# Side work of an attention stage: a list of counts per step, row sums moved between stages, and the order of two kinds of side jobs exchanged

## The chip, the cores and the metric

The kernel runs on one core of one Trainium2 chip. The metric is the device time of one execution in microseconds (us), as the median of several runs. Five engines work in parallel, each through its own queue in order: TensorE (PE in the profile; PEld is its weight load), VectorE (DVE), ScalarE (ACT), GpSimd (POOL) and SyncE (SP), which here issues most transfers.

## The reference

One inference step of two layers over 128 context tokens and 512 latent tokens, width 1024, in float32. Layer 0 is gated grouped-query attention (16 query heads, 4 key heads, head size 64), layer 1 a bidirectional gated linear recurrence. Each layer first modulates its input with shift and scale from a conditioning vector, and multiplies its output by a gate from the same vector:

```python
def _adaln(cond, w, b):
    mod = jax.nn.silu(cond.astype(jnp.float32)) @ w.astype(jnp.float32) + b.astype(jnp.float32)
    mod = mod.astype(cond.dtype)
    return jnp.split(mod, 3, axis=-1)
...
        sh_p, sc_p, g_p = _adaln(c_ctx, ada_w[i], ada_b[i])
        sh_s, sc_s, g_s = _adaln(c, ada_w[i], ada_b[i])
        hp = xp * (1.0 + sc_p) + sh_p
        hs = xs * (1.0 + sc_s) + sh_s
...
    q = _rms_norm(q.reshape(B, L, N_HEADS, HEAD_DIM), q_gain)
...
    gated = o.reshape(B, L, ATTN_WIDTH).astype(jnp.float32) * jax.nn.silu(g.astype(jnp.float32))
```

The change concerns three products with small results: the shift and scale of layer 1 (here called row sums), the gates of both layers (here called the gates' products), and the queries of layer 0.

## The kernel before, in words

All 640 tokens (five tiles of 128) are worked on together. Matrix products are made in three terms from a high and a low half of each operand (`whi`, `wlo`, `hhi`, `hlo`).

**Lead-in** (`lead_in`, L753). After the keys and values, PE makes the first of four query chunks (256 columns, four heads) and then the attention's SiLU gate path: 16 half tiles of 24 matmuls each over 320 tokens (`feat_mms`, L346, L853), four weight chunks (6 to 9) of four half tiles. After each half tile ScalarE writes its SiLU (L854). Between the half tiles stand the steps that norm, rotate and split the first queries (`q_job`, L803, ending in L694, which PE's transposes L702 read) and split the keys (`k_split`). Also after each half tile stands one job of row sums (L861) as long as there are any.

**Row sums** (`ada_cols`, L331). A job is one of 16 pieces, a 128x1024 slice of the transposed weight of layer 1's shift and scale. VectorE multiplies it with the SiLU of each of the two conditioning vectors, spread over the partitions in `silb`, and sums along the row: two instructions, L335. The product itself goes to a place that nobody reads (`spill`). Twelve of the 16 jobs are in the lead-in, with raw pieces in two buffers of their own (`adaraw`, loaded at L840 on SP's queue, the first two ahead, each further one when a job is done) and the spill in a part of `gs` that is written last. The last four (`COLS_LATE`) come later, with pieces from the common ring of three raw buffers and the spill in a ring of two slots (`s2`) that the key and query splits use too.

**Gates' products** (`ada_gen`, L315). For each layer four steps of 16 small matmuls (L284) with an add on VectorE (L321), then four small stores to memory. For layer 0 the result is then read back, spread over the partitions, into `gate0` (`gate_load`, L311), which takes over the memory of `silb`; the output projection of layer 0 needs it (L1174).

**Attention** (`att_gen`, L1001) has 36 units, nine for each of the four query chunks; each has steps that make scores, transpose probabilities and apply them to the values. Beside it runs the side work (`Side`, L60): query chunks 1, 2 and 3 (`q_gen`, L713), weights of the output projection, and splits of the attention's result. Each query chunk has a filler that it steps at places of its own: the last four jobs of row sums in chunk 1, the products of gate 0 in chunk 2, those of gate 1 in chunk 3 (L1125). `weave` (L87) takes one step of the attention, then side steps at a fixed rate of 0.62 a step. Before the first scores of a chunk, all that is left of its query chunk is forced (`side.until`, L1013).

**What sets the order.** All up to L1248 is one block whose instructions a planner puts in order on each engine: the source's order is the priority, but an instruction whose inputs are ready in the planner's own model may go ahead of earlier ones. `keep_in_program_order` (`pin`) ties an instruction to the one written before it on its engine; adaraw's loads are pinned on SP. `issue_after(ins)` puts what is written inside it behind `ins` in the queue of the engine of `ins`; elsewhere in the kernel it is given an instruction of the same engine as what is tied. The loads of raw pieces follow one list (`order`, L395 to L402), two pieces ahead (`pump`, L197).

## Time and profile before

| what | value |
|---|---|
| median of 3 runs | 842.29 us (842.24 to 848.55) |
| the profiled execution | 844.78 us |
| its span in the profile | 843.0 us |
| mean granted clock of TensorE | 0.99 |
| TensorE busy | 808.0 us of the span |
| VectorE, ScalarE, GpSimd busy | 559.9, 386.5, 215.8 us |
| row sums in the lead-in, in the attention | 24 and 8 instructions |
| gates' products | 128 matmuls, from 190.1 to 286.1 us |

The span runs from the first to the last instruction; the execution's own time has a little around it. Times in the rows are in us from the start of the span. In a row of the order of time stand start, duration, engine, line, operation, output and inputs, shape and count; in brackets the idle time of the engine before it and what ended that. In a table of windows stand the length and the busy time of each engine with its number of instructions, then the clock that TensorE was granted (1.00 is full), the share of the transfer engines and GB/s. Matmuls overlap, so their durations add up to more than the time they take.

### The profile page before, as it was taken

What the parts mean: (1) busy time and instruction counts of PE and PEld (TensorE: products, weight loads), DVE (VectorE), ACT (ScalarE), POOL (GpSimd) and SP (SyncE); (2) the same over time, 40 slices, a digit from 0 to 9 for tenths busy, and PEclk for the clock granted to TensorE, in tenths of its full rate; (3) what the DMA queues carried; (4) which work ended last, traced back from release to release, by engine and by line L of the source; (5) the groups of instructions that cost most, each with busy time, mean ns of one, the idle gap of its engine ahead of it and who ended that gap; (6) DMA issues with size and microseconds to landing.
All of it is one profiled execution on the core that took longest, in us unless ns stands there. A gap on an engine that the chain in (4) does not pass through costs nothing.

```text
span 843.0 us, 19206 instructions
## 1 busy us (share of the span) xinstructions
PE 808.0 (96%) x8025; PEld 729.2 (87%) x8025; DVE 559.9 (66%) x996; ACT 386.5 (46%) x782; POOL 215.8 (26%) x261
## 2 busy tenths in 40 slices
PE   8999899989999988999999999999999999999994
PEld 6789799878878766888999999999999999998774
DVE  4568882795657674776438575767668575858477
ACT  2252354674656776222434444435434544445232
POOL 0123001443344833010001304143333314121121
PEclk9999899999999999999999999999999999999998
DMA  9944451114151230630322322231322312324041
GB/s 325 397 145 165 151 175 52 51 54 148 51 200 51 101 100 1 225 125 35 108 69 68 103 72 82 83 109 51 107 89 83 99 61 89 120 65 157 23 161 75
DMA packets 34326, 93.28 MB, mean 111 GB/s; under 512 B 5040, under 2 KB 12224, under 8 KB 34240
## 3 DMA queue, kind: packets, MB, share of 16 engines
q1 hardware_dynamic: 23568, 74.10, 25.9%
q0 software_dynamic: 4768, 14.18, 5.4%
q10 hardware_dynamic: 5904, 3.78, 1.5%
q8 instruction: 63, 1.03, 0.5%
q14 instruction: 23, 0.19, 0.1%
HBM read 82.85 MB, written 9.19 MB: 109 GB/s over the span
## 4 chain that ended last, share of the span: by engine, by line
PE 82%; DVE 9%; ACT 2%; DMA 2%; issue 2%; POOL 1%; SPq 0%; DVEq 0%; ACTq 0%; POOLq 0%
PE rps L1319 7%; PE rps L1320 7%; PE rps L1321 7%; PE vgps L1309 5%; PE vgps L1311 5%; PE vgps L1310 5%; PE pot L896 4%; PE outp L1158 4%; PE outp L1160 3%; PE outp L1159 3%; PE pt L982 3%; PE lv L1452 2%; PE acc L536 2%; PE gps L349 2%; PE sc L869 2%
## 5 line engine op out<-in xcount | busy, mean ns | idle before, releaser
L1319 PE MATMUL rps<-h1hi,rhi 128*128 128x320 f32 x368 | 118.4, 322 | 0.0
L1320 PE MATMUL rps<-h1lo,rhi 128*128 128x320 f32 x368 | 113.9, 309 | 0.0
L1321 PE MATMUL rps<-h1hi,rlo 128*128 128x320 f32 x368 | 113.8, 309 | 0.0
L975 POOL TENSOR_SCALAR p<-p,rc 128x640 f32<-128x640 f32 x64 | 58.8, 921 | 116.6 <-DVE rc L974 102.3
L1319 PEld LDWEIGHTS rps<-h1hi,rhi 128*128 128x128 f32 x368 | 69.2, 188 | 1.3
L1320 PEld LDWEIGHTS rps<-h1lo,rhi 128*128 128x128 f32 x368 | 69.3, 188 | 0.0
L1321 PEld LDWEIGHTS rps<-h1hi,rlo 128*128 128x128 f32 x368 | 69.1, 188 | 0.0
L241 DVE TENSOR_TENSOR rlo<-raw,rhi 128x1024 fp32r<-128x1024 f32 x32 | 45.0, 1409 | 33.8 <-ACT rhi L240 33.8
L964 DVE TENSOR_REDUCE nm<-sc 128x1 f32<-128x640 f32 x64 | 52.0, 818 | 23.2 <-PE sc L870 22.8
L1480 POOL COPY At<-near 32x160 f32<-32x160 f32 x32 | 14.0, 438 | 196.8 <-DVE near L1442 195.8
L969 ACT ACTIVATE p<-sc,nm 128x640 f32<-128x640 f32 x64 | 51.2, 802 | 27.2 <-DVE nm L964 19.3
L240 ACT CAST rhi<-raw 128x1024 fp32r<-128x1024 f32 x32 | 33.6, 1049 | 52.0 <-PE rps L1320 48.8
L1430 ACT COPY kc<-A 128x640 f32<-128x640 f32 x40 | 32.2, 806 | 54.4 <-DVE A L1461 50.5
L1309 PE MATMUL vgps<-rhi,h1hi 128*128 128x256 f32 x180 | 51.5, 286 | 0.0
L1310 PE MATMUL vgps<-rlo,h1hi 128*128 128x256 f32 x180 | 50.9, 283 | 0.0
L1311 PE MATMUL vgps<-rhi,h1lo 128*128 128x256 f32 x180 | 50.9, 283 | 0.0
L982 PE MATMUL pt<-small,p 128*128 128x128 f32 x320 | 48.6, 276 | 1.4 <-ACT pts L874 0.9
L869 PE MATMUL sc<-kk,X 128*128 128x320 f32 x128 | 42.6, 343 | 6.1 <-ACT p L969 6.0
L874 ACT COPY pts<-pt 128x512 f32<-128x512 f32 x64 | 35.8, 591 | 24.4 <-PE pt L982 24.1
L982 PEld LDWEIGHTS pt<-small,p 128*128 128x128 f32 x320 | 37.1, 140 | 7.8 <-issue 5.3
L1309 PE MATMUL vgps<-wspare,h1hi 128*128 128x256 f32 x140 | 41.8, 298 | 0.0
L896 PE MATMUL pot<-pts,vv 128*64 128x256 f32 x320 | 38.9, 386 | 2.4 <-DVE pts L874 2.4
(301 smaller groups left out, 2423.6 us busy)
## 6 DMA issues: line engine op xcount, KB each, us to landing
raw<-in_rec_w_in SPq DMA_DIRECT2D x40, 512.0 KB, 3.7
raw<-in_ada_m SPq DMA_DIRECT2D x16, 512.0 KB, 8.0
raw<-in_attn_w_in SPq DMA_DIRECT2D x16, 512.0 KB, 4.2
raw<-in_ada_s SPq DMA_DIRECT2D x16, 512.0 KB, 4.4
adaraw<-in_ada_c SPq DMA_DIRECT2D x12, 512.0 KB, 3.8
raw<-in_attn_w_out SPq DMA_DIRECT2D x8, 512.0 KB, 4.1
raw<-in_rec_w_out SPq DMA_DIRECT2D x8, 512.0 KB, 3.5
x1d<-y SPq DMA_DIRECT2D x5, 512.0 KB, 2.6
```

The source lines that it names most:

```text
L869: nc.tensor.matmul(out, X[:, h, t0:t0 + P], kk[:, c, k0:k1], start=True, stop=False)
L896: nc.tensor.matmul(pot[j * HD:(j + 1) * HD, :CW], vv[:, slot, c * HD:(c + 1) * HD], moving[j], start=first, stop=last)
L964: nc.vector.tensor_reduce(nm[:, 0:1], sc[:, :, :320], AX.XY, ALU.max, negate=True)
L969: return nc.scalar.activation(halves(p[:]), sc[:, :, :320], AF.Exp, bias=nm[:, 0:1], accum_out=su[:, 0:1])
L975: nc.gpsimd.tensor_scalar(p, p, rs[:, 0:1], 1.0, ALU.mult, ALU.mult)
L982: nc.tensor.transpose(pt[:, i * 256 + q * P:i * 256 + (q + 1) * P], ps[q][:, (k0 + i) * P:(k0 + i + 1) * P], ident)
L1309: nc.tensor.matmul(out, h1hi[:, k, t], hi, start=(k == 0), stop=False)
L1310: nc.tensor.matmul(out, h1hi[:, k, t], lo, start=False, stop=False)
L1311: nc.tensor.matmul(out, h1lo[:, k, t], hi, start=False, stop=(k == KT - 1))
L1319: nc.tensor.matmul(ps[:, j, :320], hi[:, k, :], h1hi[:, k, t], start=(k == 0), stop=False)
L1320: nc.tensor.matmul(ps[:, j, :320], hi[:, k, :], h1lo[:, k, t], start=False, stop=False)
L1321: nc.tensor.matmul(ps[:, j, :320], lo[:, k, :], h1hi[:, k, t], start=False, stop=(k == KT - 1))
```

## The change

1. In the lead-in, eleven jobs of row sums and not twelve. They are made by a generator that stops after each of a job's two sums. `ROWS_AT` says how many sums stand after each half tile: none after the first four, one after the fifth and sixth, two after the seventh to fifteenth; what is left follows the last. Each sum stands in an `issue_after` with the latest SiLU. The spill is in `gs` up to the twelfth half tile, then in the `s2` ring. The next raw piece is still loaded when a job is done.
2. The five other jobs go beside query chunk 3, one sum a step; then comes the load of `gate0`. The products of gate 0 go beside chunk 1 and those of gate 1 beside chunk 2; the list of loads is exchanged alike.
3. `FILL_AT` says at which places of a query chunk its filler is stepped: the token tile of the unit and a letter for the half of a token tile after which it stands, or `e` for the end of the unit. Before, it was one step at the start of chunks 2 and 3, one in each unit, and the rest at the end.
4. `SIDE_AT` is a digit for each of the attention's 189 steps: the number of side steps behind it, in place of the rate 0.62.

```diff
+FILL_AT = {1: '0a0b0e2e4e', 2: '0b0e2e4e', 3: '0b0e4e'}
...
-SIDE_B = 0.62
+SIDE_AT = (
+    "0101101011111000110110101101011011010110111001101021010010110110"
+    "1001011010210101200101002011110100110101101002011000121110001101"
+    "0110110101101002002110010110101101102002011101000001201101011")
...
-COLS_LATE = 4
+COLS_LATE = 5
+ROWS_AT = (0, 0, 0, 0, 1, 1, 2, 2, 2, 2, 2, 2, 2, 2, 2, 0)
...
-def weave(main, side, ratio):
-    acc = 0.0
-    for _ in main:
-        acc += ratio
-        while acc >= 1.0:
-            acc -= 1.0
+def weave(main, side, steps):
+    for n, _ in enumerate(main):
+        for _ in range(int(steps[n]) if n < len(steps) else 1):
             side.step()
...
         yield
-        if layer == 0:
-            gate[0] = gsp.tile([P, 2, D], F32, tag="gate", name="gate0")
-            gate_load(0, nc.gpsimd)
-
-    def ada_cols(job, raw, spill):
+
+    def ada_cols(job, raw, spill, after):
...
         for c in range(2):
-            nc.vector.scalar_tensor_tensor(spill, raw, 1.0, silb[:, c, :], ALU.mult, ALU.mult,
-                                           accum_out=shsc[1][:, s, ft, c:c + 1])
+            with tc.issue_after(after()) if after else ExitStack():
+                nc.vector.scalar_tensor_tensor(spill(), raw, 1.0, silb[:, c, :], ALU.mult, ALU.mult,
+                                               accum_out=shsc[1][:, s, ft, c:c + 1])
+            yield
...
+    def spare():
+        return prep.tile([P, D], F32, tag="s2", name="spill", bufs=2)
+
     def cols_gen():
         for job in COLS[len(COLS) - COLS_LATE:]:
-            ada_cols(job, take(("ada_c",) + job), prep.tile([P, D], F32, tag="s2", name="spill", bufs=2))
+            yield from ada_cols(job, take(("ada_c",) + job), spare, None)
             pump()
-            yield
+        gate[0] = gsp.tile([P, 2, D], F32, tag="gate", name="gate0")
+        gate_load(0, nc.gpsimd)
...
-        order.extend(ada_pieces(c - 1) if c else [("ada_c",) + job for job in COLS[len(COLS) - COLS_LATE:]])
+        order.extend(ada_pieces(c) if c < 2 else [("ada_c",) + job for job in COLS[len(COLS) - COLS_LATE:]])
...
-        if c > 1:
-            next(fill)
-            yield
+        spots = {FILL_AT[c][i:i + 2] for i in range(0, len(FILL_AT[c]), 2)}
         pend = None
         for tt0, n in UNITS:
-            ps = yield from tok_unit(w, tt0, n, "qmm")
+            ps = None
+            gen = tok_unit(w, tt0, n, "qmm")
+            step = 0
+            while ps is None:
+                try:
+                    next(gen)
+                except StopIteration as e:
+                    ps = e.value
+                    break
+                step += 1
+                yield
+                if f"{tt0}{'0abcd'[step]}" in spots:
+                    next(fill, None)
+                    yield
...
-            next(fill, None)
-            yield
+            if f"{tt0}e" in spots:
+                next(fill, None)
+                yield
...
+        silus = []
+
+        def spill():
+            return gs[:, KT - 2:, :].rearrange("p a b -> p (a b)")[:, :D] if len(silus) <= 12 else spare()
+
+        def cols_steps():
+            while raws:
+                yield from ada_cols(*raws.popleft(), spill, lambda: silus[-1])
+                cols_load()
+
+        cgen = cols_steps()
...
-                    nc.scalar.activation(gs[:, 2 * (ch - 6) + mt, t0:t1], ps[:, :320], AF.Silu)
+                    silus.append(nc.scalar.activation(gs[:, 2 * (ch - 6) + mt, t0:t1], ps[:, :320], AF.Silu).ins)
...
-                    if raws:
-                        ada_cols(*raws.popleft(), gs[:, KT - 2:, :].rearrange("p a b -> p (a b)")[:, :D])
-                        cols_load()
+                    for _ in range(ROWS_AT[step - 1]):
+                        next(cgen, None)
...
-        assert not raws
+        drain(cgen)
...
-        yield from q_gen(c, Xs[c], ada_gen(c - 2) if c > 1 else cols_gen())
+        yield from q_gen(c, Xs[c], ada_gen(c - 1) if c < 3 else cols_gen())
...
-    weave(att, side, SIDE_B)
+    weave(att, side, SIDE_AT)
```

## The prediction

> **What bounds the kernel now.** I read the page's busy shares, then busy time by stretch, then the chain of waits, then single engines in order of time.

> ```profile
> PE 808.0 (96%) x8025; PEld 729.2 (87%) x8025; DVE 559.9 (66%) x996; ACT 386.5 (46%) x782; POOL 215.8 (26%) x261
> PE 82%; DVE 9%; ACT 2%; DMA 2%; issue 2%; POOL 1%; SPq 0%; DVEq 0%; ACTq 0%; POOLq 0%
> ```

> TensorE is the bound: 808.0 of 843.0 us busy, 82% of the chain. The change touches none of its work, so it can only win back idle time, 35 us in all, and only in the stage it edits. The next rows show that stage: two pieces of the lead-in, then the attention, cut about where its query chunks are made (first, second and last chunk, then what follows).

> ```profile
> 86.24:91.78 5.54, 1.39 (x11) 1.07 (x9) 5.54 (x11) 1.70 (x4) 0.00 (x0) 0.73 0.43 155
> 91.78:97.10 5.32, 5.32 (x24) 5.32 (x25) 5.32 (x10) 2.10 (x3) 0.00 (x0) 0.64 0.21 85
> 141.00:190.00 49.00, 44.44 (x351) 38.71 (x349) 42.11 (x95) 32.08 (x72) 23.01 (x21) 1.00 0.18 58
> 190.00:240.00 50.00, 49.43 (x429) 40.66 (x429) 31.33 (x71) 29.16 (x66) 19.97 (x23) 1.00 0.32 114
> 240.00:292.00 52.00, 50.64 (x440) 42.43 (x439) 33.82 (x71) 32.14 (x74) 30.56 (x32) 1.00 0.33 112
> 292.00:338.00 46.00, 39.94 (x293) 29.46 (x293) 26.95 (x58) 32.75 (x70) 18.15 (x22) 1.00 0.15 47
> ```

> After each window's length come the busy times of PE, weight load, DVE, ACT and POOL, then the granted clock. PE idles 4.15 us in the first window and runs at a clock of 0.64 in the second. It idles 4.56 us beside the first chunk, where DVE has its fullest stretch (42.11 of 49), 0.57 beside the second, 1.36 beside the last and 6.06 after it.

> **Part 1: the row sums leave the first four half tiles.** DVE's order of time, the transposes that wait for it, and the loads:

> ```profile
> 82.45 0.69 DVE L615 TENSOR_TENSOR qn<-pmm,rq 128x512 f32<-128x512 f32 x1 [0.85 <-POOL rq L191]
> 83.06 1.21 DVE L335 SCALAR_TENSOR_TENSOR gs<-adaraw,silb 128x1024 f32<-128x1024 f32 x1
> ...
> 85.40 1.22 DVE L335 SCALAR_TENSOR_TENSOR gs<-adaraw,silb 128x1024 f32<-128x1024 f32 x1
> ...
> 87.75 1.22 DVE L335 SCALAR_TENSOR_TENSOR gs<-adaraw,silb 128x1024 f32<-128x1024 f32 x1
> ...
> 89.49 0.69 DVE L694 TENSOR_TENSOR qs<-r,qs 128x512 fp32r<-128x512 f32 x1
> ```
> ```profile
> 90.33 1.23 PE L702 MATMUL qps<-identr,qs 128*128 128x128 f32 x8 [3.92 <-DVE qs L694]
> ...
> 98.27 0.80 PE L702 MATMUL qps<-identr,qs 128*128 128x128 f32 x8
> ```
> ```profile
> 58.75 0.90 SPq L840 DMA_DIRECT2D adaraw<-in_ada_c  x2
> 62.64 11.67 SPq L219 DMA_DIRECT2D raw<-in_attn_w_in  x2
> 76.05 13.28 SPq L840 DMA_DIRECT2D adaraw<-in_ada_c  x4
> 89.38 8.68 SPq L219 DMA_DIRECT2D raw<-in_attn_w_in  x2
> ```
> ```profile
> 82.92 0.44 ACT L854 ACTIVATE gs<-gps 128x320 f32<-128x320 f32 x1 [3.08 <-PE gps L351]
> 86.44 0.44 ACT L854 ACTIVATE gs<-gps 128x320 f32<-128x320 f32 x1 [3.08 <-PE gps L351]
> ```

> The first query tile's chain (82.45 to 89.49) has three row sums between its links; PE's transposes stand in its in-order queue and wait 3.92 us for the last link. Then PE is slow: a half tile takes 86.44 - 82.92 = 3.52 us, but 5.32 in the window at clock 0.64, 1.80 more. The eight transposes take 1.23 against 0.80, and 0.2 of idle follows: 0.6. This place costs 3.92 + 1.80 + 0.6 = 6.3 us.

> ROWS_AT begins the first pair of sums at half tiles 5 and 6. SP's queue holds this up: the third adaraw load is now written in half tile 7, behind the weight pieces which now issue at 89.38 to 98.06, perhaps 6 us earlier without the stall. So job 3 cannot run before about 92. Only the four sums of jobs 1 and 2, whose data come with the loads of 58.75, could run earlier. The chain without the three sums: each holds DVE some 1.15 us, 3.5 us together; the last link then ends near 86.3, PE being ready at 86.24. Gain 6.3; bounds: 0, if the four sums take the places of the three, and 6.3.

> I count nothing on the tie: it names a Silu, on ACT, while the sums run on DVE, and issue_after orders only what shares the named instruction's engine. If it were a true wait, DVE would stand behind a Silu up to a half tile (3.52 us), and with it the key splits and PE's transposes after them.

> Nine jobs follow from about 92 until the attention starts. Two sums a half tile at 1.23 are 2.45 of 3.52 us; DVE's spare time there hides them (0.82 busy between 130 and 140, one row below). The extra buffer for the last sums shares its slots with the key splits: cost nothing while that spare time is there; if it is gone, the attention's first maxima are late by a sum, 1.2 us.

> ```profile
> 130.00:140.00 10.00, 10.00 (x72) 9.99 (x71) 0.82 (x1) 3.90 (x9) 0.00 (x0) 1.00 0.01 2
> ```

> **Part 2: the first chunk gets products for row sums.** The chain of waits in this stretch, and the sums and products by themselves:

> ```profile
> 144.42 1.21 DVE spill L335 x2
> ...
> 146.37 1.14 DVE spill L335 x2
> ...
> 182.76 1.33 DVE spill L335 x2
> ...
> 185.55 1.15 DVE spill L335 x2
> 186.72 3.35 DMA raw<-in_ada_s
> ```
> ```profile
> L335 DVE SCALAR_TENSOR_TENSOR spill<-raw,silb x8: 1208/1214/1747, 144.3 to 185.5; 128x1024 f32<-128x1024 f32 x8
> ```
> ```profile
> 200.26 1.07 PE L284 MATMUL adaps<-raw,sil 128*32 128x256 f32 x16
> ...
> 273.92 0.42 DVE L321 TENSOR_TENSOR acc<-acc,adaps 128x256 f32<-128x256 f32 x1
> ```

> Four of the eight sums lie on the chain, 4.83 us. They go, and four products of sixteen matmuls (1.07 us each) come: PE's 4.3 us fill into its 4.56 of idle time, DVE falls from 42.11 by 8 x 1.3 and rises by four adds of 0.42, to about 33 of 49. The products only move: first chunk +4.3, second as before (ada1 for ada0), last chunk -4.3. So the stretch stays near 49 and the last one loses 4.3. Bounds: 0 if the idle time is the start of the softmax and not DVE, 4.56 if all goes. I take 4.3, since the sums are on the chain.

> The products' loads come earlier in SP's queue, behind the eleventh adaraw load; bounds 0 and one landing (4.4, below) for each of four steps. I take 0: the planner places a product where it expects its data.

> **Part 3: ten sums beside the last chunk.** DVE there goes from 33.82, less 4 x 0.42, plus 10 x 1.23, to 44.4 of about 47.7 us. Seven of them are written behind the last query split, six steps being forced at its deadline (two before). But DVE's order is not the source's: modA, written behind the whole attention, runs where its data are ready:

> ```profile
> 190.89 0.16 DVE L1090 TENSOR_TENSOR modA<-shsc,lnc 128x16 f32<-128x16 f32 x1
> ```
> ```profile
> PE qps L702 <- DVE qs L694: 1.0, 1, 1.0
> ```

> So sums spread into DVE's gaps from when their raws land. The cost lies between 0 and the first chunk's 4.83 us. The nearest row is the stretch's own: PE once waits 1.0 us there for DVE. I add one more such wait: +1.0. Whoever waits behind a sum: maxima, reciprocals and probability copies, then ACT's exponentials and PE.

> The gate load moves to the end of these sums; POOL issues it, and its data are needed only at the output projection, past 338: nothing, while some 40 us lie between. Its issue waits for the last sum, and POOL's scalings queue behind it; at one sum at most, inside the 1.0.

> **Part 4: counts and places.** I stepped both orders through: the same attention steps, the same deadlines, side steps moved by one or two places. After the last chunk there is no query product left to fill PE, so its 6.06 us stay. I take 0, bounds -4 (two thirds of that idle time) and +3 (about half as much again as PE idles beside the three chunks, 4.56 + 0.57 + 1.36 = 6.5).

> **The sum.** -6.3 - 4.3 + 1.0 + 0 = -9.6 us. The profiled execution took 844.78 us (span 843.0 and 1.8 around it), so 835.2; it lay 2.5 above the median of 842.29, so as a median 832.7.

> [...] DVE beside POOL:

> ```profile
> L335 DVE SCALAR_TENSOR_TENSOR gs<-adaraw,silb x24: 1214/1224/1226, 71.6 to 122.0; 128x1024 f32<-128x1024 f32 x24
> ```
> ```profile
> L975 POOL TENSOR_SCALAR p<-p,rc x64: 788/800/2217, 143.8 to 330.2; 128x640 f32<-128x640 f32 x64
> ```

> Where POOL is idle (the lead-in) all 24 sums take 1.21 to 1.23; beside POOL's scalings one of eight took 1.747, and a scaling grew from 0.800 to 2.217. POOL is fuller in the last chunk (30.56 of 52) than in the first (23.01 of 49). [...]

> **Rivals.** First, the last chunk gives back what the first gains: DVE at 93% there, and ten sums against scalings that take up to 1.4 us longer. Part 3 costs the first chunk's 4.83 and not 1.0: 832.7 + 3.8 = 836.5. For it: the swap is nearly symmetrical. Against: DVE has 18 us to spare there, and X3 does not wait for a sum.

> Second, the row sums are not held back: with a void tie the planner puts jobs 1 and 2 into the chain's gaps. Then the stall stays and only parts 2 and 3 count: 842.29 - 3.3 = 839.0. Against: those four now run before 82.45, while DVE waits for POOL's rq.

> Third, slower: the products come too early for their data. Loads queue on SP behind adaraw loads that wait for sums, and PE's queue is in order:

> ```profile
> raw<-in_ada_s SPq DMA_DIRECT2D x16, 512.0 KB, 4.4
> ```

> If each of the first chunk's four steps waits a whole landing of 4.4 us, 17.6 - 9.6 = +8.0: 850.3. It decides from 2.4 us a step. For it: the chain already has 3.35 of such a load at 186.72. Against: that load waited for a sum's buffer, which no longer stands before a product.

> Fourth, the counts also clear part of what follows the last chunk, part 4 at -4: 828.7.

> **How the numbers follow.** Main 0.55 at 832.7, its own range 829.5 to 836; first rival 0.18, second 0.08, third 0.06, fourth 0.13. A measurement of this kernel can tell about 1% from no change, 833.9 and 850.7 here. Main lies below 833.9 in about two of three cases (0.37); with the fourth 0.50 faster. Slower by over 1% is half of the third and a little for what I miss: 0.04. The rest, 0.46, is within 1%. The range 828 to 840 leaves out the third rival and the edges of the others.

> **What would show it.** Part 1: the wait of qps for qs near 86 to 90 gone, clock 1.00 through the lead-in, no adaraw sum of job 3 before 92; wrong if the wait is still over 1 us. Part 2: PE idle beside the first chunk under 1.5 us with adaps there, no spill on its chain. Part 3: PE idle beside the last chunk under 2.5; wrong if spill rows stand on its chain for over 2 us. Part 4: idle after it still 5 to 7. The forecast is wrong above all if the lead-in's stall returns at another link, such as the key splits.

## The result, and the profile after

The changed kernel takes 838.25 us as a median of 7 runs (836.37 to 839.39), the kernel before 845.39 in the runs beside it. The ratio is 0.9918, with a 95% interval of 0.9899 to 0.9938: faster by 0.8%. The three runs from which the forecast started (842.29) lay low; the sets of runs beside the experiments had medians of 845.09, 843.66, 844.46 and 845.31. So the fair comparison is by ratio: forecast 835.2 / 844.78 = 0.9886, measured 0.9918; or -9.6 us forecast, -6.9 measured.

The page of the changed kernel, busy shares and the chain:

```profile
PE 806.7 (97%) x8025; PEld 727.9 (87%) x8025; DVE 563.3 (67%) x996; ACT 386.6 (46%) x782; POOL 212.5 (25%) x261
PE 82%; DVE 9%; issue 3%; ACT 2%; DMA 1%; POOL 1%; SPq 0%; DVEq 0%; ACTq 0%; POOLq 0%
```

TensorE is the bound as before. To see where the time went, both traces are cut at the same events: first and last matmul of the half tiles, last transposes of the first, second and last query chunk, first matmul of the output projection. The kernel before, then the changed one; columns as in the prediction's windows:

```profile
72.17:140.78 68.61, 64.46 (x448) 64.00 (x447) 48.65 (x79) 27.99 (x53) 4.47 (x1) 0.95 0.40 131
140.78:187.32 46.54, 43.01 (x342) 37.55 (x342) 39.65 (x89) 31.19 (x70) 22.14 (x19) 1.00 0.15 47
187.32:237.59 50.27, 48.66 (x423) 40.82 (x423) 32.11 (x75) 27.83 (x63) 19.86 (x23) 1.00 0.35 122
237.59:292.34 54.75, 53.39 (x462) 43.99 (x463) 36.06 (x74) 34.55 (x79) 31.88 (x33) 1.00 0.32 111
292.34:336.82 44.48, 38.42 (x284) 28.13 (x282) 26.15 (x57) 31.57 (x69) 16.79 (x20) 1.00 0.15 48
336.82:843.00 506.18, 492.21 (x5496) 459.23 (x5496) 336.18 (x546) 209.17 (x412) 107.50 (x150) 0.99 0.30 94
```
```profile
71.49:134.50 63.01, 62.58 (x448) 62.05 (x447) 46.39 (x75) 27.87 (x53) 4.47 (x1) 1.00 0.38 135
134.50:183.94 49.44, 48.49 (x410) 40.01 (x410) 33.65 (x80) 30.47 (x68) 21.40 (x24) 1.00 0.28 97
183.94:232.55 48.61, 48.44 (x416) 40.36 (x414) 31.86 (x68) 28.57 (x66) 18.78 (x22) 1.00 0.32 112
232.55:284.02 51.47, 47.99 (x386) 41.95 (x387) 38.85 (x79) 34.64 (x79) 28.19 (x27) 1.00 0.09 30
284.02:328.62 44.60, 39.29 (x298) 28.89 (x296) 35.26 (x73) 31.64 (x69) 19.96 (x22) 1.00 0.32 118
328.62:835.60 506.98, 492.44 (x5496) 459.20 (x5496) 336.25 (x546) 209.23 (x412) 106.80 (x150) 0.99 0.29 94
```

Row by row: half tiles -5.60, first chunk +2.90, second -1.66, last -3.28, after it +0.12, all that follows +0.80. A window's length less its PE time is PE's idle time: the first chunk's falls from 3.53 to 0.95, but its PE time rises by 5.48, so the stage grows. In the last chunk PE time falls by 5.40, but idle time rises from 1.36 to 3.48. A stage need not hold the same work in both kernels: of the last chunk's 92 matmuls on the values (`pot`) 80 are left in the changed kernel, and 12 run in the stretch after it, whose count rises by 14.

The lead-in went as the prediction drew it. DVE's order and SP's queue in the changed kernel:

```profile
81.66 0.69 DVE L620 TENSOR_TENSOR qn<-pmm,rq 128x512 f32<-128x512 f32 x1 [2.19 <-POOL rq L193]
82.38 0.69 DVE L659 TENSOR_TENSOR u<-qn,sinq 128x512 f32<-128x512 f32 x1
82.99 0.69 DVE L661 TENSOR_TENSOR r<-qn,cosq 128x512 f32<-128x512 f32 x1
83.71 0.69 DVE L663 TENSOR_TENSOR r<-r,u 128x512 f32<-128x512 f32 x1
85.09 0.69 DVE L699 TENSOR_TENSOR qs<-r,qs 128x512 fp32r<-128x512 f32 x1 [0.69 <-ACT qs L698]
...
97.16 1.23 DVE L335 SCALAR_TENSOR_TENSOR gs<-adaraw,silb 128x1024 f32<-128x1024 f32 x1 [1.16 <-DMA adaraw<-in_ada_c]
```
```profile
58.07 0.90 SPq L857 DMA_DIRECT2D adaraw<-in_ada_c  x2
61.84 29.91 SPq L221 DMA_DIRECT2D raw<-in_attn_w_in  x4
91.80 0.90 SPq L857 DMA_DIRECT2D adaraw<-in_ada_c  x2
```

No sum stands between the links of the first query tile; the last link ends at 85.78 (forecast 86.3), of the transposes' wait 0.2 us is left, and the clock is 1.00. The third adaraw load issues at 91.80, so job 3's first sum runs at 97.16.

### The profile page after: what moved, and what is told of

Read it like the earlier page. It is cut to its first block, busy times and chain, and to the rows that moved or that the text cites. A ratio compares the mean times of both kernels' runs of the same rounds, so it can differ in the third digit from the quotient of the medians.

```text
span 835.6 us, 19217 instructions
## 1 busy us (share of the span) xinstructions
PE 806.7 (97%) x8025; PEld 727.9 (87%) x8025; DVE 563.3 (67%) x996; ACT 386.6 (46%) x782; POOL 212.5 (25%) x261
## 3 DMA queue, kind: packets, MB, share of 16 engines
q8 instruction: 63, 1.03, 0.5%
## 4 chain that ended last, share of the span: by engine, by line
PE 82%; DVE 9%; issue 3%; ACT 2%; DMA 1%; POOL 1%; SPq 0%; DVEq 0%; ACTq 0%; POOLq 0%
PE rps L1346 7%; PE rps L1347 7%; PE rps L1348 7%; PE vgps L1336 5%; PE vgps L1338 5%; PE vgps L1337 5%; PE outp L1185 4%; PE pot L923 4%; PE outp L1187 3%; PE outp L1186 3%; PE pt L1009 3%; PE lv L1479 2%; PE acc L541 2%; PE sc L896 2%; PE qmm L364 2%
## 5 line engine op out<-in xcount | busy, mean ns | idle before, releaser
L1002 POOL TENSOR_SCALAR p<-p,rc 128x640 f32<-128x640 f32 x64 | 56.1, 880 | 128.8 <-DVE rc L1001 106.5
L1507 POOL COPY At<-near 32x160 f32<-32x160 f32 x32 | 13.5, 422 | 195.1 <-DVE near L1469 194.1
L354 PE MATMUL gps<-hhi,whi 128*128 128x320 f32 x128 | 40.0, 312 | 0.1
## 6 DMA issues: line engine op xcount, KB each, us to landing
raw<-in_rec_w_in SPq DMA_DIRECT2D x40, 512.0 KB, 3.6
raw<-in_ada_m SPq DMA_DIRECT2D x16, 512.0 KB, 8.1
raw<-in_attn_w_in SPq DMA_DIRECT2D x16, 512.0 KB, 4.5
raw<-in_ada_s SPq DMA_DIRECT2D x16, 512.0 KB, 4.0
adaraw<-in_ada_c SPq DMA_DIRECT2D x11, 512.0 KB, 5.3
raw<-in_attn_w_out SPq DMA_DIRECT2D x8, 512.0 KB, 3.3
raw<-in_rec_w_out SPq DMA_DIRECT2D x8, 512.0 KB, 3.5
raw<-in_ada_c SPq DMA_DIRECT2D x5, 512.0 KB, 4.4
```

Source lines behind the costliest of these rows:

```text
L1002: nc.gpsimd.tensor_scalar(p, p, rs[:, 0:1], 1.0, ALU.mult, ALU.mult)
```

## The experiments

All lengths between the same events, in us, PE's idle time after the slash; "sum" is from the first half tile to the output projection. They come from one profiled execution each. The stretches ahead and behind, which no edit of these touches on purpose, differ by up to 3.8 and 1.6 us between profiles, so a stage is compared, and the ratio (with its interval) tells the whole. In some of these executions TensorE's clock also fell to 0.50 for 3.41 us, which by the estimate in the last section takes up to 1.7 us from a stage. Outside the half tiles such a fall stands in chunk 1 of lead_only and lead_and_list, in chunk 3 of own_spill, at the end of chunk 3 or behind it in swap_counts, rate_not_list, loads_unpinned, split_products and tail_products, and one of twice the length in chunk 2 of lead_thin_11. The changed kernel's profile has none.

| run | half tiles | chunk 1 | chunk 2 | chunk 3 | after it | sum | ratio to before |
|---|---|---|---|---|---|---|---|
| before | 68.61/4.15 | 46.54/3.53 | 50.27/1.61 | 54.75/1.36 | 44.48/6.06 | 264.65 | 1 |
| changed | 63.01/0.43 | 49.44/0.95 | 48.61/0.17 | 51.47/3.48 | 44.60/5.31 | 257.12 | 0.9918 [0.9899, 0.9938] |
| lead_only | 63.13/0.59 | 50.48/5.46 | 50.22/1.56 | 54.63/1.36 | 44.44/6.05 | 262.90 | 0.9977 [0.9958, 0.9995] |
| swap_counts | 68.12/4.19 | 49.31/1.03 | 48.33/0.17 | 51.48/3.50 | 44.98/4.25 | 262.22 | 0.9979 [0.9962, 0.9997] |
| lead_and_list | 63.19/0.63 | 50.21/5.46 | 50.41/1.69 | 53.43/0.98 | 44.28/3.24 | 261.52 | 0.9933 [0.9907, 0.9959] |
| rate_not_list | 63.42/0.82 | 49.44/0.95 | 48.70/0.39 | 52.79/2.75 | 44.34/5.35 | 258.69 | 0.9924 [0.9897, 0.9950] |
| loads_unpinned | 71.13/7.27 | 49.45/0.95 | 48.58/0.16 | 51.72/3.51 | 44.44/4.39 | 265.32 | 1.0023 [1.0007, 1.0039] |
| before_thin | 68.64/4.03 | 46.14/2.59 | 49.28/1.26 | 54.65/1.38 | 44.21/5.80 | 262.92 | 0.9995 [0.9983, 1.0007] |
| lead_thin | 62.98/0.43 | 48.81/4.20 | 48.71/0.70 | 54.92/1.44 | 44.46/6.04 | 259.88 | 0.9953 [0.9934, 0.9972] |
| lead_thin_11 | 63.36/0.80 | 45.07/1.25 | 53.94/3.32 | 54.77/1.38 | 44.47/6.06 | 261.61 | 0.9967 [0.9944, 0.9990] |
| own_spill | 63.12/0.55 | 49.07/0.71 | 48.32/0.17 | 55.22/3.11 | 44.50/4.35 | 260.22 | 0.9943 [0.9916, 0.9971] |
| thin_late | 63.23/0.67 | 49.45/0.95 | 48.58/0.16 | 51.03/2.14 | 46.15/5.96 | 258.44 | 0.9944 [0.9930, 0.9959] |
| split_products | 62.98/0.43 | 49.44/0.94 | 47.44/0.80 | 54.80/1.38 | 46.10/6.02 | 260.76 | 0.9969 [0.9955, 0.9982] |
| tail_products | 63.28/0.76 | 49.45/0.95 | 47.47/0.79 | 52.00/3.75 | 46.64/4.25 | 258.84 | 0.9949 [0.9930, 0.9969] |

**1. One part alone: lead_only.** The kernel before with the new lead-in (twelve jobs, none exchanged, rate 0.62):

```diff
-                    if raws:
-                        ada_cols(*raws.popleft(), gs[:, KT - 2:, :].rearrange("p a b -> p (a b)")[:, :D])
-                        cols_load()
+                    for _ in range(ROWS_AT[step - 1]):
+                        next(cgen, None)
```

> The lead-in's new row sums alone: all of the attention's side work as before (rate 0.62, four late jobs beside chunk 1, gate products beside chunks 2 and 3), twelve jobs in the lead-in after the new list. Theory: the lead-in's stall was the larger part of the gain by itself; half tiles 68.6 us before, 63.0 with the change, so 5.6 us less, ratio to before 0.9934, and beside the first chunk PE idles 3.5 us as before. Rival: the lead-in's gain is given back at the first chunk, whose VectorE now starts late; ratio over 0.998.

The stall went (63.13), but the first chunk took 3.94 of the 5.5 us back. Theory fell: the lead-in's gain is not kept by itself. DVE at the border:

```profile
133.50 1.23 DVE L338 SCALAR_TENSOR_TENSOR spill<-adaraw,silb 128x1024 f32<-128x1024 f32 x1 [0.63 <-DMA adaraw<-in_ada_c]
134.66 1.22 DVE L338 SCALAR_TENSOR_TENSOR spill<-adaraw,silb 128x1024 f32<-128x1024 f32 x1
135.80 1.23 DVE L243 TENSOR_TENSOR wlo<-raw,whi 128x1024 fp32r<-128x1024 f32 x1
```
```profile
PE qmm L366 <- DVE wlo L243: 1.9, 1, 1.9
```

The twelfth job's load is late, its two sums run into the attention, and behind them stands the low half of the first chunk's weights, for which PE waits 1.9 us; a stretch at low clock follows (0.50 for 3.41 us, last section). These two make up the 3.94 us: the chunk has 342 matmuls as before, 1.93 us more idle time and 2.01 us more PE time.

**2. The other parts alone: swap_counts**, the changed kernel with a whole job after each of the first eleven half tiles, as before.

> The exchange of side jobs and the list of counts alone, with a job after each of the first eleven half tiles as before. Theory: transposes wait for qs by about 4 us again and the clock falls, half tiles about 68.6 us; only the attention's part is left, 1.9 us, ratio 0.998. Rival: the order beside the chunks is what counts and the stall is hidden later; ratio 0.994 or less.

Confirmed: the wait of the transposes is back (3.8 us), and without the lead-in only 0.2% is left (a fall of the clock behind chunk 3 has a part in that).

**3. The exchange undone: lead_and_list**, lead_only with the list of counts.

> The changed kernel with the exchange undone: late jobs beside chunk 1, gate products beside 2 and 3, old places of the filler, but new lead-in and the list of counts. Theory: the exchange brings the first chunk its gain and costs the last chunk what the sums do there; without it PE idles about 3.5 us beside the first chunk and about 1.4 beside the last, total ratio 0.9935. Rival: exchange and list gain only together; then the attention stage is no shorter than before, 196 or more, ratio 0.9935 to 0.996; or the exchange costs more than it gains, ratio under 0.991.

The first chunk is as long as in lead_only, and the four stages of the attention take 198.3 us (196.0 before), as the rival had it; the ratio is the theory's. By the ratio this run is nearer to the changed kernel than its sum says (-5.7 against -3.1 us); the intervals of the two kernels overlap, so the exchange's worth on top is 4.4 us by the stages (up to 1.7 of it a fall of the clock) and not resolved by the times.

**4. The list undone: rate_not_list**, the changed kernel with the rate of 0.62.

> The changed kernel with the rate of 0.62 in place of the list of counts. Theory: the list is worth nothing by itself (0, from -4 to +3 in the prediction), ratio to before 0.992, attention stage within 1.5 us of the changed kernel's 194.1. Rival: the list carries the attention's gain; the stage takes 196 or more, ratio 0.995.

Confirmed: 1.6 us by the stages, which is about what the fall of the clock behind chunk 3 takes there, and nothing that the times can tell.

**5. What keeps the sums back: loads_unpinned.**

```diff
-                pin(nc.sync.dma_start(raw, piece(("ada_c",) + cols[0])))
+                nc.sync.dma_start(raw, piece(("ada_c",) + cols[0]))
```

> The changed kernel, but the loads of the lead-in's ada_c rows may be issued wherever the planner likes, not only in the written order. Theory (SP's written order, not the tie to the half tiles, keeps the row sums out of the first query tile's chain): the third load moves ahead of weight pieces, sums stand between the chain's links again, PE's transposes wait 2.5 to 4.5 us for the first split, the sixteen half tiles take 66.5 to 68.5 us in place of 63.0, and the ratio is 0.996 to 0.999. Rival (it is enough that the sums are written behind half tiles 5 and later): the half tiles stay at 63 to 64 us, no such wait over 1 us, ratio 0.991 to 0.993.

The sums come forward and the stall returns, larger than expected. The same chain in this kernel, and what PE does:

```profile
88.53 0.68 DVE L620 TENSOR_TENSOR qn<-pmm,rq 128x512 f32<-128x512 f32 x1
89.13 1.21 DVE L335 SCALAR_TENSOR_TENSOR gs<-adaraw,silb 128x1024 f32<-128x1024 f32 x1
...
91.48 1.22 DVE L335 SCALAR_TENSOR_TENSOR gs<-adaraw,silb 128x1024 f32<-128x1024 f32 x1
...
93.22 1.22 DVE L335 SCALAR_TENSOR_TENSOR gs<-adaraw,silb 128x1024 f32<-128x1024 f32 x1
...
94.37 0.68 DVE L699 TENSOR_TENSOR qs<-r,qs 128x512 fp32r<-128x512 f32 x1
```
```profile
95.20 1.32 PE L707 MATMUL qps<-identr,qs 128*128 128x128 f32 x8 [7.14 <-DVE qs L699]
```

Again three sums between the links, and more ahead of them, which also push the first link from 81.66 to 88.53 (2.25 us of that the half tiles as a whole start later). `ROWS_AT` and the tie are as in the changed kernel, so neither keeps the sums back by itself: SP's written order of loads does, in which `ROWS_AT` has put the third load behind the weight pieces. The tie holds nothing: sums written after the fifth half tile and later run here from 61.47 on, while the first half tile starts at 73.74.

**6. What idles PE beside the first chunk: before_thin.** The kernel before with the eight sums over 8 of 1024 columns (the rest is left out):

```diff
-            ada_cols(job, take(("ada_c",) + job), prep.tile(...))
+            ada_cols(job, take(("ada_c",) + job)[:, :8], prep.tile(...))
```

> The kernel before with its eight sums beside the first chunk over 8 of 1024 columns; the other columns are left out. Theory (PE's idle time beside the first chunk is made by these sums): the first chunk falls from 46.54 us to 43 to 44, its idle time from 3.53 to under 1, all else stays, ratio 0.996. That would mean that the sums and the products share one idle time: taking the sums away uses it up, and the products that come in their place find nothing to fill and cost their 4.3 us in full. Rival (the idle time is the softmax's start, which the products can fill): the first chunk stays at 45.5 us or more with over 2.5 us idle, ratio 0.999.

```profile
140.23:186.37 46.14, 43.55 (x346) 38.16 (x346) 34.04 (x95) 31.18 (x70) 19.88 (x20) 1.00 0.17 57
186.37:235.65 49.28, 48.02 (x418) 40.19 (x419) 31.07 (x69) 27.86 (x63) 19.12 (x22) 1.00 0.33 113
```
```profile
PE sc L869 <- ACT p L969: 1.9, 4, 0.9
PE pot L896 <- DVE pts L874: 0.6, 1, 0.6
```

The rival is right: DVE is 5.6 us less busy there (34.04 against 39.65), and the chunk is 0.4 us shorter, the next one 1.0. PE waits for ScalarE's exponentials all the same. The four sums lay on the chain with 4.83 us; taken away, other work took their place. (Thin sums still hold their raw buffers, so this tests their time on DVE alone.)

**7. What took the lead-in's gain back: lead_thin**, lead_only with thin sums beside the first chunk, and then **lead_thin_11**, in which eleven jobs stand in the lead-in and five thin ones beside the chunk.

> The kernel of lead_only (the new lead-in alone, four jobs still beside the first chunk) with these eight sums over 8 of 1024 columns; the other columns are left out. There the first chunk had taken back 3.94 of the 5.5 us that the lead-in gave. Theory (what takes it back is not the eight sums but the softmax's start and the lead-in's last sums, which now end later beside the attention; in before_thin the sums were worth 0.4 us): the first chunk stays at 49 to 50.5 us with 4 to 5.5 us of PE idle, ratio 0.997 to 0.998. Rival (the eight sums take it back): the chunk falls to 46 to 47.5 us with under 3 us idle, ratio 0.993 to 0.995.

Between theory and rival: the chunk is 1.67 us shorter than in lead_only and the next one 1.51. That is not all the sums' worth, since the clock, which fell in lead_only's first chunk, stayed at 1.00 here. Against before_thin, the fair partner, the new lead-in is now worth 3.0 us by the sums of the stages (262.92 to 259.88) and not 1.75, with 2.6 of its 5.7 still missing; PE's wait for the weights' low half stays, 2.4 us.

> The kernel of lead_thin, but eleven jobs (22 sums) in the lead-in and five beside the first chunk, these again over 8 of 1024 columns; the other columns are left out. In lead_only and lead_thin the load of the twelfth job lands near 133.4 and 135.2 us, its two sums end two and a half us later, and behind them on DVE stands the low half of the first chunk's weights, for which PE waits 1.9 and 2.4 us. Theory (what the lead-in gained is given back by that twelfth job): the wait of qmm for wlo is gone, the first chunk falls from 48.81 to 46 to 47.3 us with 2 to 3 us of PE idle, and the ratio is 0.9925 to 0.994. Rival (the first chunk waits for its softmax, and without products to fill in it stays long): the chunk stays at 48.3 us or more, idle over 3.5, ratio 0.995 or above.

The wait for `wlo` is gone, and the chunk falls further than expected, to 45.07; but the second chunk grows by 5.2. The theory was right on the wait and wrong on the time. The second chunk's window, its start in the chain, and what PE does there:

```profile
181.23:235.17 53.94, 50.62 (x419) 42.35 (x419) 32.10 (x72) 28.92 (x64) 18.94 (x22) 0.94 0.33 116
```
```profile
179.31 0.58 DVE spill L338 x2
179.91 5.28 DMA raw<-in_ada_s
```
```profile
185.23 1.08 PE L286 MATMUL adaps<-raw,sil 128*32 128x256 f32 x8 [2.95 <-DMA raw<-in_ada_s]
```

The sums, thin as they are, still hold the raw buffers until the chunk's end, so the second chunk's first product load issues at 179.91 and PE waits 2.95 us for it, and then runs slowly (0.94 over the stage). SP's queue in the changed kernel:

```profile
135.71 15.27 SPq L221 DMA_DIRECT2D raw<-in_ada_s  x6
151.08 17.66 SPq L221 DMA_DIRECT2D raw<-in_attn_w_in  x2
170.16 26.72 SPq L221 DMA_DIRECT2D raw<-in_ada_s  x7
```

There a product's buffer is free again when PE has read it: the first chunk's last product ends at 170.11, and SP, waiting for it, issues the next load at 170.16. The second chunk's loads then issue from 170.16 on, 13.8 us ahead of that chunk, and PE never waits for one.

**8. Where the late sums stand: own_spill.** Their unused product goes to a tile of their own (in bfloat16, as only that is free; the sums stay in float32).

```diff
-            yield from ada_cols(job, take(("ada_c",) + job), spare, None)
+            yield from ada_cols(job, take(("ada_c",) + job), lambda: lspill[0], None)
```

> The ten late sums write their unused products into a tile of their own (bfloat16, since only that much room is free), instead of the two slots they share with the query splits. Theory (the shared slots hold the sums back): in the changed kernel the last eight of the ten run at 265 to 294, one beside each split, and PE's transposes wait 2.0 to 2.6 us three times for a split behind a sum. With a tile of their own the sums run as soon as their rows of ada_c have landed, the most of them before the first split of the last chunk; of the three waits at most one is left, the last chunk falls from 51.47 to 48.5 to 50 us, and the ratio to the kernel before is about 0.989. Rival (the sums cost DVE's time beside the last chunk, wherever they stand): ten sums in a row push the softmax's maxima and the first tile's chain, the waits only move, the chunk stays at 51 to 53 and the ratio at 0.992 or above.

First the changed kernel's late sums (durations in ns, then first and last start), and a place where one hurts; then own_spill's. Of the three waits of the transposes that the expectation names, the trace has this one.

```profile
L335 DVE SCALAR_TENSOR_TENSOR spill<-raw,silb x10: 1197/1210/2604, 233.2 to 293.3; 128x1024 f32<-128x1024 f32 x10
```
```profile
280.35 2.60 DVE L335 SCALAR_TENSOR_TENSOR spill<-raw,silb 128x1024 f32<-128x1024 f32 x1
```
```profile
280.32 1.55 POOL L1134 TENSOR_TENSOR hlo<-gs,hhi 128x640 fp32r<-128x640 f32 x1
```
```profile
283.50 0.52 PE L707 MATMUL qps<-identr,qs 128*128 128x128 f32 x4 [2.44 <-DVE qs L699]
```
```profile
L335 DVE SCALAR_TENSOR_TENSOR lspill<-raw,silb x10: 1203/1222/1724, 233.0 to 256.8; 128x1024 bf16<-128x1024 f32 x10
```
```profile
231.75:286.97 55.22, 52.11 (x394) 43.30 (x394) 44.91 (x94) 33.47 (x78) 29.89 (x29) 0.97 0.25 83
```
```profile
PE sc L896 <- ACT p L996: 2.3, 2, 1.9
PE pt L1009 <- ACT pts L901: 0.7, 1, 0.7
```

On the order the theory is right: with their own tile all ten run by 258 and the wait of the transposes is gone. On the time the rival is: ten sums close together push the softmax instead (waits of 1.9 and 0.7 near 247), the clock falls (0.57 from 248 to 252), and the stage is 3.75 us longer. Its idle time is no longer than the changed kernel's (3.11 against 3.48): what grew is PE's time, by 4.12, of which up to 1.7 is the clock; 8 more matmuls stand in the stage, and the rest was not traced. The two shared slots held the sums back, and that did no harm.

**9. What the late sums cost: thin_late**, the changed kernel with its ten late sums over 8 columns (the rest is left out; the edit is that of before_thin).

> The changed kernel with its ten late sums over 8 of 1024 columns, so that they cost almost nothing but keep their place and their buffers; the sums' other columns are left out. Theory (what part 3 costs is DVE time of sums in front of splits): the waits of 2.0 to 2.6 us fall to about 1, the last chunk goes from 51.47 to 48 to 49.5 us with less than 1.5 us of PE idle in place of 3.48, and what follows it keeps its 5 to 6 us of idle; ratio about 0.988. Rival (the sums are covered, and the waits come from the softmax's own length or the planner's order): the last chunk stays above 50.5 us and the ratio is 0.991 or above.

The 2.4 us wait is gone, the idle time falls to 2.14, but the chunk is only 0.44 us shorter and the stretch behind it 1.55 longer. The rival holds on the time: the sums' time on DVE costs nothing that can be measured. It does not hold on the wait, which went with the sums' time; but 8 more matmuls stand in the chunk than in the changed kernel, so the planner's order is not quite the same either.

**10. Two tries for more: split_products** moves two of the second chunk's product steps beside the last chunk (and two jobs of sums the other way), **tail_products** moves them behind it.

```diff
+        order.extend((ada_pieces(0), s1[:2] + late[:2] + s1[2:4], s1[4:] + late[2:])[c])
...
-        yield from q_gen(c, Xs[c], ada_gen(c - 1) if c < 3 else cols_gen())
+        yield from q_gen(c, Xs[c], (None, ada_gen(0), mix2(), mix3())[c])
```

> The changed kernel, but the last two of the second chunk's four product steps go beside the last chunk, and two of the five late jobs go beside the second. Theory (products pay only where PE is idle for want of the softmax: 0.17 us beside the second chunk, 3.48 beside the last): the second chunk falls by 1.6 to 2.5 us from 48.61, the last grows by at most 1 from 51.47 with under 2 us idle left, ratio to the kernel before about 0.990. Rival (the idle time beside the last chunk is not such as a product can fill): what the second chunk loses the last gains, their sum stays within 0.5 us of 100.1, ratio 0.992.

> As split_products, but these two product steps go behind the last chunk, where PE idles 5.31 of 44.6 us and has no other matmuls to fill in. Theory (products fill idle time of the softmax): the second chunk falls by 1.6 to 2.5 us, the stretch after the last chunk grows by at most 1 us, its idle time falls to 2.5 to 4; sum from the lead-in to the output projection 1 to 2 us less than the changed kernel's 257.1, ratio about 0.990. Rival (four more loads stand in SP's queue before the output weights, and the products take a bank from the softmax): the stretch grows by 2.5 us or more and nothing is won, ratio 0.992 to 0.994.

Both second chunks fell by just 1.2 us, and the last chunk with what follows it grew by 4.8 and 2.6. In split_products idle time did fall there, 3.48 to 1.38, and the stage was longer all the same. In both, the clock fell at the end of the last chunk or behind it (0.96 and 0.97 over the stretch behind it), in tail_products after the same wait of 2.44 us that left it at 1.00 in the changed kernel; up to 1.7 us of the growth is that. Without it tail_products would be about level with the changed kernel by the stages. Neither beats it.

## Why the prediction was right or wrong

**Part 1, right, the size 0.7 too high** (-5.6 against -6.3): 3.72 of it is idle time and 1.88 PE's time at the low clock, where the prediction had 4.1 and 2.2. (So the change can win back more than idle time, against the prediction's opening; and its 86.3 for the last link does not come out of its rows, 89.49 + 0.69 - 3.5 = 86.7.) The void tie and SP's order as what keeps the sums back are shown by run 5, job 3 not before 92 by its first sum at 97.16, and the four early sums ran from 70.79 to 79.4, before the chain, as it said.

What the prediction did not see is that most of this gain is lost when the lead-in is changed alone: by the ratios it brings 1.9 us, the exchange with the list 1.8, both together 6.9. That the whole is more than the sum, by 3.2 us, is only just clear of the noise. By the stages it is -1.75, -2.43 and -7.53, but there up to 1.7 us on each of the first two is a fall of the clock that the changed kernel's profile was spared. With the list added (lead_and_list) the ratio cannot be told from the changed kernel's. Two causes of the loss are shown, each by a wait of PE and a slow clock behind it: the twelfth job ahead of the first chunk's weights, and sums that hold buffers the products need. Run 7 thins the sums and takes the twelfth job away, and against before_thin still keeps only 1.3 us, since the buffers stay held; whether freeing them earlier would keep the rest was not tried.

**Part 2, the step that failed: "PE's 4.3 us fill into its 4.56 of idle time".** It expected 0 in the first chunk, which grew by 2.90, though the sign that it named, idle time under 1.5 us, came true (0.95). Two errors lie in it. The 4.56 came from a window that ran to 190 and took in the beginning of the second chunk; the first chunk's own idle time is 3.53, and of that 2.58 was filled. And the products took more than 4.3, since two of the four steps were split into groups of 8 and 8, and 10 and 6, which took 0.64 and 0.64, and 1.05 and 0.63 us, in place of 1.07 for sixteen in a row: here are the groups of the changed kernel's first chunk and of the last chunk before,

```profile
L286 PE MATMUL adaps<-raw,sil 128*32 128x256 f32 x64 | 5.1, 388 | 0.0
```
```profile
L284 PE MATMUL adaps<-raw,sil 128*32 128x256 f32 x64 | 4.3, 385 | 0.0
```

and four score matmuls of the next chunk came into the stage as well. The reason given, that the sums are on the chain, is refuted by run 6: the idle time is the softmax's, as in the prediction's own lower bound, "0 if the idle time is the start of the softmax and not DVE". But that bound is refuted too, since the products filled most of it. Against the growth stands a gain that the prediction had put at zero: the second chunk's -1.66, since its product loads no longer wait for a sum's buffer (PE's wait of 1.15 us for one at 190.11 is gone). Over both chunks PE's time rose by 5.26 and its idle time fell by 4.02, so the two cost 1.24. Of rival 3, products too early for their data, nothing is seen: no product of the changed kernel waits for a load.

**Part 3, right in size, wrong in how.** The last chunk's -3.28 meets -4.3 + 1.0, but by luck in its terms: PE's time fell by 5.40 and not 4.3, as 12 matmuls moved behind the chunk, and idle time rose by 2.12 and not 1.0. With the stretch after it, where that work went, the terms are -4.53 and +1.37, together -3.16. Nor did ten sums run beside the chunk: four did, and six ran behind it, from 284.35 to 293.29, where DVE's time rises from 26.15 to 35.26 us and PE had idle time in any case. And "sums spread into DVE's gaps from when their raws land" is not what they do: the raws of jobs 2 to 4 have landed by 241.9, and their sums start from 265.1 to 288.7 (run 8 shows why); and the idle time of 3.48 is above the 2.5 that the prediction allowed. One sum stands in front of a split, and PE waits 2.44 us; run 9 shows that removing this brings 0.4 us. The first rival, that the last chunk gives back the first chunk's 4.83, did not occur. The total could not show it, since that rival's 836.5 is a ratio of 0.9931 and lies in the measured interval; the stages do.

**DVE beside POOL.** One of the ten late sums took 2.604 us against 1.21, and began within 0.03 us of a POOL split that took 1.55: one after the other the two are 2.76, and the pair took 2.63 (280.32 to 282.95). Four more sums overlap an instruction of POOL, and each time one of the two is longer: the sums at 265.14 and 291.24 take 1.29 and 1.38 us, and two scalings of POOL, at 285.80 and 288.89, take 1.62 against 0.80. The five sums that met none took 1.21 to 1.23. In the lead-in two sums, at 76.97 and 78.23, ran beside one instruction of POOL (4.47 us from 77.15) and took 1.22. Why one of the two is longer beside the last chunk was not shown. The longest sum is the one with PE's wait behind it, yet thin_late shows that it decides nothing; so scalings longer by 0.82 us were there, and the first rival, which counted on up to 1.4, did not follow.

**Part 4, right** (+0.12 after the last chunk, 5.31 idle; run 4 puts the list at 1.6 us over all stages, about one fall of the clock). What follows the output projection's start was no term at all and costs 0.80; runs with sums beside or behind the last chunk, ten or six, have 495.2 to 496.0 us from there to PE's end, those without 494.4 to 494.7. These are also the runs that load `gate0` behind the sums; why was not tested.

The miss of 2.7 us is made up of 0.7 in part 1, 1.3 in parts 2 and 3 (-2.04 against -3.3), 0.1 in part 4 and 0.8 behind: 2.9 by the profiled executions, of which 0.7 comes back in the stretch ahead of the half tiles, which no term covers. The main case's own range, 829.5 to 836, is 0.9848 to 0.9925 of the 842.29 it started from, so 0.9918 lies near its upper end. The even chance given to a gain of over 1% did not come true. The profiled execution of the changed kernel had no fall of the clock in these stages, so its stages show it at its best.

## What to carry to other kernels

Idle time of the bound engine is counted between the same events in both kernels, not in round windows: the same microsecond was here counted for two stages. Work that lies on the chain need not be what the stage waits for: thin it to a few columns and see whether the stage shortens before you build on it. When a stall goes, look at what the freed engine or buffer meets next, since two edits can each be worth little and be worth nearly twice their sum together. Before a stage of one execution is compared, see whether the clock fell in one of the two.

## What the runs showed of the hardware

```profile
134.88:138.29 3.41, 1.55 (x13) 1.35 (x13) 3.41 (x6) 1.38 (x3) 0.35 (x1) 1.00 0.18 43
138.29:141.70 3.41, 3.41 (x18) 3.41 (x17) 3.38 (x9) 1.15 (x4) 3.18 (x2) 0.50 0.57 174
```
```profile
282.06:285.47 3.41, 0.96 (x7) 0.73 (x8) 3.41 (x7) 1.89 (x5) 2.15 (x3) 1.00 0.00 0
285.47:288.88 3.41, 3.41 (x20) 2.23 (x18) 3.41 (x7) 1.37 (x3) 1.64 (x2) 0.50 0.78 244
```
```profile
279.14:282.55 3.41, 1.93 (x14) 1.49 (x12) 3.41 (x5) 3.04 (x8) 2.73 (x3) 1.00 0.00 0
282.55:285.97 3.42, 2.46 (x22) 2.18 (x24) 3.42 (x10) 1.91 (x5) 1.05 (x2) 1.00 0.45 158
```

In tail_products the wait lies within one window, PE is busy for 0.96 of its 3.41 us, and the clock is 0.50 in the next. In the changed kernel the same wait lies across two windows, PE is busy for 1.93 and 2.46 us, and the clock stays at 1.00; so here the length of the wait did not decide. In rate_not_list no wait there was over 0.9 us, and the clock fell (busy 1.79 of 3.41). In the kernel before, the window ahead of the fall at 88.74 and the first of the fall itself have PE busy for 1.07 and 1.61 us; no other from 25 to 815 us has under 2.07, and no other has a fall behind it. In the changed kernel, with no fall there, none has under 1.93. So among the windows given here the clock fell behind those with PE busy for 0.96 to 1.79 us of 3.41, and behind none with 1.93 or more; what sets it was not shown.

For pricing a stall here (an estimate from the clock of 0.50 in these windows): half of what PE works in the slow stretch goes to the clock, 1.7 us in lead_only (3.41 us busy) and 2.5 in the kernel before (5.02 busy in 6.83).
